# VectorE in a fixed order in the output projection, spatial gating in matmuls of 256 columns, LayerNorm stages further apart

## The chip, the core and the metric

The kernel runs on one core of a Trainium2 chip. Five engines matter here: TensorE (PE in the profile, with its weight loads as PEld), VectorE (DVE), ScalarE (ACT), GpSimd (POOL) and SyncE (SP), which issues all the DMAs of this kernel. The metric is the device time of one execution in microseconds; lower is better. Each engine works through its own list of instructions in order, and an instruction that must wait for another engine holds up everything behind it on its own.

## The reference

One layer of a streaming encoder with two branches of 512 channels each, over a prompt of 2048 frames and a sample of 32 frames. D_MODEL is 1024, all in float32.

```python
h = jnp.einsum('bsd,de->bse', x, w_in)            # 1024 -> 6 * 512
u, v, ga, bv, bg, gb = jnp.split(h, [...], axis=-1)
u = jax.nn.gelu(u, approximate=False)
v = layer_norm(jax.nn.gelu(v, approximate=False), a_ln_g, a_ln_b)
y_a = u * spatial_gating(v, a_ws, a_bias) * jax.nn.silu(ga)
a = bv * jax.nn.sigmoid(bg)
c, new_hist = depthwise_causal_conv(conv_hist, a, b_conv_w, b_conv_b)   # width 31
y_b = jax.nn.silu(layer_norm(c, b_ln_g, b_ln_b)) * jax.nn.silu(gb)
y = jnp.einsum('bse,ed->bsd', jnp.concatenate([y_a, y_b], axis=-1), w_out)
x_new = layer_norm(ALPHA * x + y, post_ln_g, post_ln_b)
```

`spatial_gating` multiplies each chunk of 128 positions, for each of 8 heads of 64 channels, by a lower triangular 128 x 128 matrix and adds a bias per position. The outputs are the new x of prompt and sample, the last 30 rows of the convolution's input of both, and the normalised v of the sample.

## The kernel before

*Precision.* TensorE is fed with a 32-bit format that rounds. So every operand is split into a high part (a rounding copy on ScalarE) and a low part (the difference, mostly on GpSimd, line 74, or VectorE, line 68), and a product is three matmuls: high by high, high by low, low by high. Splitting is much of ScalarE's and GpSimd's work.

*Stages.* The frames stand in four groups of 512 columns (the second has the 32 sample frames besides). They are treated in two halves p of two groups each. A half runs, in this order: v of its first group (`mm_v`, lines 328 to 330), the projections bg and bv (`mm_f`, lines 301 and 304), v of its second group, then u, ga and gb. Behind them comes the output projection (`o_tile`, `o_sample`, `o_product`, all through `mm`, line 664).

*The order of work.* A planner puts the instructions of each engine in an order ahead of time, by a due time that `when(t)` sets and by its own estimate of when operands are ready; a buffer is given out when its holder has been read for the last time. One unit of t is 12 matmuls of 512 columns. `chain(t, ...)` gives each of several functions a due time one unit after the last; `at(t, fn)` calls a function when the loop has come to t. `tc.issue_after(i)` fixes that what follows is queued behind i on the same engine. `mm` does so for every matmul of the output projection; the other engines' order there is the planner's.

*Spatial gating.* `ev_v` takes v of a group through GELU and its LayerNorm, splits it (tiles vh and vl, line 558), and lets `spat(u, two)` run for each pair of chunks u and each parity `two` of the heads: four heads, three matmuls of 128 columns each (line 573, weights from v, moving operand wth or wtl, the split triangular matrices), into one bank of PSUM, which ScalarE empties into S with two copies (line 578), one for each chunk. The sample's chunk takes 32 rows and 32 columns (tile wts). Units are two t apart.

*Branch B.* `conv` runs as chains of scalar-tensor-tensor instructions on VectorE (line 71). `ln_chain` then takes each group through six stages: sums of the channels, mean (by matmuls with ones, lines 441 and 442), squares, deviation and reciprocal, scaling (z), and SiLU with the gate (sw, gates). They are given to `chain`, one unit apart.

*Split of x.* `split_x` splits the transposed x; its low part is on VectorE for group 0 and on GpSimd for the others (line 183).

*Output projection.* The first two of eight units of 256 rows and the sample are plain products. Units 2 to 7 use a Strassen-like scheme of seven products in place of eight (`PRODUCTS`): of the blocks A11, A12, A21, A22 of y (unit's rows by channels) with S1 = A21 + A22, S2 = S1 - A11, S3 = A11 - A21, S4 = A12 - S2. Each product is 12 matmuls of 512 columns. Products 1, 3, 5 and 7 of a unit add up in one bank (oA), 2 in oB, 4 and 6 in oC. After each product VectorE reads the bank into the rows r of the result, so the next product into oA may start only when VectorE has read the one before. `load_yraw` brings the blocks of y from DRAM; `y_block` makes the four sums on VectorE (S2 is written over A11, so it waits until A11 is split), and splits each block for TensorE, five blocks ahead of use. `finish` then normalises each tile of 128 rows: inverse deviation by a power on GpSimd, r scaled and shifted on ScalarE, times the gain on VectorE, plus the bias on GpSimd, and the store.

In the last unit the first of its two tiles is finished in halves, one half on VectorE and one on GpSimd, and the last one in VectorE alone.

Of the kernel before, what the change touches and what calls it, by code (L numbers as in the profile page):

```python
# [15 lines left out]
P = 128  # L16
# [28 lines left out]
def hymba_step_kernel(ctx, tc, xT, xn, xs_n, wall, wsT, abias, vecs, avec, post, cache,  # L45
# [132 lines left out]
    def split_x(g, k):  # L178
        t = sb.tile([P, 2, WMAX], F32R, name=f"xs{g}_{k}", tag="xs", bufs=20)
        r = xraw.pop((g, k))  # L180
        w = GW[g]
        nc.scalar.copy(t[:, 0, :w], r[:, :w])  # L182
        (tt if g == 0 else gtt)(t[:, 1, :w], r[:, :w], f(t[:, 0, :w]), SUB)
        xsp[g, k] = t
# [41 lines left out]
    wts = sb.tile([NS, 2, 8, NS], F32R, name="wts", tag="pg", bufs=1)  # L226
# [26 lines left out]
    def setup_order():  # L253

        wm = setup["wm"]
        nc.scalar.copy(wts[:, 0], wm[:NS, :, :NS])
        tt(wts[:, 1], wm[:NS, :, :NS], f(wts[:, 0]), SUB)
# [4 lines left out]
    def setup_hi():  # L262
        for a in range(2):
            nc.scalar.copy(wt[0][:, :, 64 * a : 64 * a + 64], setup["wm"][:, :, a:P:2])

    def setup_lo():
        for a in range(2):
            c = slice(64 * a, 64 * a + 64)
            tt(wt[1][:, :, c], setup["wm"][:, :, a:P:2], f(wt[0][:, :, c]), SUB)

    def setup_bias():
        bb = setup["bb"]
        for h4 in range(2):
            p = bank(f"wsum{h4}")
            sl = slice(4 * h4, 4 * h4 + 4)
            nc.tensor.matmul(p, one1, wt[0][:, sl], start=True, stop=False)
            nc.tensor.matmul(p, one1, wt[1][:, sl], start=False, stop=True)
# [168 lines left out]
    def ln_chain(g, h):  # L446
# [45 lines left out]
        def run():  # L492
# [10 lines left out]
            chain(h, *fns)  # L503
# [23 lines left out]
    def ev_v(g, res):  # L527
# [33 lines left out]
        def spat(u, two):  # L561
# [3 lines left out]
            if (u, two) == (0, 0):  # L565
                S[g] = sb.tile([P, 4, WMAX], F32, name=f"S{g}", tag="S", bufs=2)
            p = bank(f"sp{g}_{u}_{two}")
            for pr in range(4):
                h = 2 * pr + two
                hi, lo = [x[:m, h, : len(ch), :] for x in sp[u]]  # L570
                o = p[:w, P * pr : P * pr + P]
                for m3, (l, r) in enumerate(((hi, 0), (hi, 1), (lo, 0))):
                    nc.tensor.matmul(o[:, :m], l, wt[r][:, h] if m == P else wts[:, r, h],  # L573
                                     start=(pr + m3 == 0), stop=(m3 == 2), skip_group_check=True)
# [90 lines left out]

    def load_wo(k, dh):
# [23 lines left out]
    def load_y(u):  # L690

        g, c0 = u // 2, 256 * (u % 2)
        for j in range(4):
# [6 lines left out]
            elif j % 2 == 0:  # L700
# [345 lines left out]
```

## Time and profile before

| | |
|---|---|
| three runs | 798.62, 802.79 and 1060.04 us, median 802.79 |
| the profiled execution | 797.06 us, of which the span from the first to the last instruction is 795.3 us |
| granted clock of TensorE, mean | 0.983 |
| chain that ended last | PE 73%, DMA 9%, DVE 7%, POOL 3% |
| matmuls of f (lines 301 and 304) | 2400, busy 591.7 us |
| matmuls of the output projection (line 664) | busy from 598.7 to 784.1 us |
| DMA | 101.18 MB, mean 127 GB/s |

Rows of groups give line, engine, operation, output <- inputs, shape and count, then busy time in us and mean ns of one, then the idle time before them. Rows in order of time give start and length in us, and in brackets the idle time of the engine just before and what ended it. Matmuls overlap, so their cost is read from one start to the next rather than from their length. Rows of windows give a stretch, its length, the busy time of PE, PEld, DVE, ACT and POOL with the number of instructions, and then TensorE's granted clock, the DMA engines' share and GB/s.

### The profile page before, as it was taken

What the parts mean: (1) busy time and instruction counts of PE and PEld (TensorE: products, weight loads), DVE (VectorE), ACT (ScalarE), POOL (GpSimd) and SP (SyncE); (2) the same over time, 40 slices, a digit from 0 to 9 for tenths busy, and PEclk for the clock granted to TensorE, in tenths of its full rate; (3) what the DMA queues carried; (4) which work ended last, traced back from release to release, by engine and by line L of the source; (5) the groups of instructions that cost most, each with busy time, mean ns of one, the idle gap of its engine ahead of it and who ended that gap; (6) DMA issues with size and microseconds to landing.
All of it is one profiled execution on the core that took longest, in us unless ns stands there. A gap on an engine that the chain in (4) does not pass through costs nothing.

```text
span 795.3 us, 10662 instructions
## 1 busy us (share of the span) xinstructions
PE 765.8 (96%) x3787; PEld 639.7 (80%) x3787; DVE 571.4 (72%) x842; ACT 303.3 (38%) x523; POOL 395.9 (50%) x337
## 2 busy tenths in 40 slices
PE   8999999999999899899999999999999999889894
PEld 6899998899889799788888888888887877678673
DVE  5449899899962667115999899984657577776675
ACT  5662332443223566463221254333546222233320
POOL 2654575545437834954132544332101565886673
PEclk9999999999989899999999999999999999999998
DMA  9631453312136733831111311123618888244112
GB/s 299 216 101 41 125 186 105 102 44 67 44 133 227 245 101 96 270 95 40 41 44 50 95 55 40 40 80 102 216 44 282 257 330 319 100 139 133 53 54 80
DMA packets 63718, 101.18 MB, mean 127 GB/s; under 512 B 8624, under 2 KB 30256, under 8 KB 63536
## 3 DMA queue, kind: packets, MB, share of 16 engines
q1 hardware_dynamic: 63664, 100.49, 38.8%
q8 instruction: 30, 0.49, 0.2%
q14 instruction: 24, 0.20, 0.1%
HBM read 74.32 MB, written 26.14 MB: 126 GB/s over the span
## 4 chain that ended last, share of the span: by engine, by line
PE 73%; DMA 9%; DVE 7%; POOL 3%; issue 3%; ACT 2%; SPq 1%; DVEq 0%; POOLq 0%; ACTq 0%
PE f L301 34%; PE f L304 17%; PE oA L664 6%; PE t L329 3%; PE t L330 3%; PE t L328 3%; DMA out_dram<-r 2%; PE sp L573 2%; DVE yr L68 2%; PE oB L664 2%; DMA yr<-yd 1%; DMA xr<-in_xT_dram 1%; DMA t3l<-td 1%; DVE gb L68 1%; DVE r L68 1%
## 5 line engine op out<-in xcount | busy, mean ns | idle before, releaser
L301 PE MATMUL f<-xs,wh 128*128 128x512 f32 (+2 forms) x1600 | 377.2, 359 | 0.0
L301 PEld LDWEIGHTS f<-xs,wh 128*128 128x128 f32 x1600 | 276.2, 191 | 41.3
L74 POOL TENSOR_TENSOR wl<-wr,wh 128x512 fp32r<-128x512 f32 x104 | 140.4, 1353 | 224.8 <-ACT wh L162 224.6
L304 PE MATMUL f<-xs,wl 128*128 128x512 f32 (+2 forms) x800 | 214.5, 357 | 0.0
L304 PEld LDWEIGHTS f<-xs,wl 128*128 128x128 f32 x800 | 144.2, 191 | 21.0
L162 ACT CAST wh<-wr 128x512 fp32r<-128x512 f32 x112 | 69.1, 620 | 183.8 <-PE f L301 84.8
L71 DVE SCALAR_TENSOR_TENSOR c<-A,hF,c 128x512 f32<-128x512 f32 x120 | 90.4, 753 | 6.3 <-ACT c L77 3.0
L71 DVE SCALAR_TENSOR_TENSOR c<-A,vec,c 128x512 f32<-128x512 f32 x120 | 89.7, 747 | 0.0
L71 DVE SCALAR_TENSOR_TENSOR c<-d,vec,c 128x512 f32<-128x512 f32 x112 | 83.6, 747 | 0.6
L329 PE MATMUL t<-wl,xs 128*128 128x512 f32 x128 | 50.3, 404 | 2.1 <-POOL wl L74 2.1
L328 PE MATMUL t<-wh,xs 128*128 128x512 f32 x128 | 48.2, 401 | 0.8 <-ACT xs L202 0.8
L330 PE MATMUL t<-wh,xs 128*128 128x512 f32 x128 | 48.3, 401 | 0.0
L74 POOL TENSOR_TENSOR r<-r,pgb 128x1024 f32<-128x1024 f32 (+1 forms) x16 | 38.4, 2402 | 17.8 <-DVE r L68 10.5
L74 POOL TENSOR_TENSOR xs<-xr,xs 128x512 fp32r<-128x512 f32 (+1 forms) x24 | 33.3, 1403 | 23.5 <-ACT xs L182 23.4
L68 DVE TENSOR_TENSOR A<-f,sg 128x512 f32<-128x512 f32 (+1 forms) x20 | 10.7, 579 | 36.6 <-PE f L304 35.4
L74 POOL TENSOR_TENSOR yl_A<-yr,yh_A 128x512 fp32r<-128x512 f32 x18 | 25.9, 1440 | 17.0 <-ACT yh_A L827 14.7
L578 ACT COPY S<-sp 64x512 f32<-64x512 f32 (+1 forms) x34 | 19.1, 562 | 35.6 <-PE sp L573 35.3
L74 POOL TENSOR_TENSOR to<-bo,to 128x256 fp32r<-128x256 f32 x32 | 26.3, 824 | 12.9 <-ACT to L361 12.8
L68 DVE TENSOR_TENSOR S<-S,ga 128x512 f32<-128x512 f32 (+1 forms) x16 | 13.8, 892 | 25.2 <-ACT ga L77 25.2
L361 ACT CAST to<-bo 128x256 fp32r<-128x256 f32 x32 | 12.9, 406 | 48.1 <-DMA td<-to 24.6
L329 PEld LDWEIGHTS t<-wl,xs 128*128 128x128 f32 x128 | 24.7, 193 | 8.0 <-POOL wl L74 2.5
L328 PEld LDWEIGHTS t<-wh,xs 128*128 128x128 f32 x128 | 24.7, 194 | 7.9 <-ACT xs L202 1.3
(179 smaller groups left out, 1200.1 us busy)
## 6 DMA issues: line engine op xcount, KB each, us to landing
wr<-in_wall_dram SPq DMA_DIRECT2D x112, 256.0 KB, 2.6
td<-to SPq DMA_DIRECT2D x32, 256.0 KB, 2.8
yr<-yd SPq DMA_DIRECT2D x64, 128.0 KB, 3.3
r<-in_xn_dram SPq DMA_DIRECT2D x16, 512.0 KB, 5.0
out_dram<-r SPq DMA_DIRECT2D x14, 512.0 KB, 2.6
xr<-in_xT_dram SPq DMA_DIRECT2D x23, 256.0 KB, 4.1
bo<-in_wall_dram SPq DMA_DIRECT2D x32, 128.0 KB, 2.8
wor<-in_wall_dram SPq DMA_DIRECT2D x16, 256.0 KB, 2.7
```

Source lines behind the costliest of these rows:

```text
L68: nc.vector.tensor_tensor(out, a, b, op=op)
L71: nc.vector.scalar_tensor_tensor(out, a, s, b, op0=op0, op1=op1)
L74: nc.gpsimd.tensor_tensor(out, a, b, op=op)
L162: nc.scalar.copy(hi, r)
L301: nc.tensor.matmul(pt[b][:, :w], hk, xsp[g, k][:, part, c0 : c0 + w], start=(k == 0 and part == 0), stop=False)
L304: order["mm"] = nc.tensor.matmul(pt[b][:, :w], lk, xsp[g, k][:, 0, c0 : c0 + w], start=False, stop=(k == NK - 1))
L328: nc.tensor.matmul(pt[t][:m], hi[:, c0 : c0 + m], wh, start=st, stop=False)
L329: nc.tensor.matmul(pt[t][:m], hi[:, c0 : c0 + m], wl, start=False, stop=False)
L330: nc.tensor.matmul(pt[t][:m], lo[:, c0 : c0 + m], wh, start=False, stop=en)
L573: nc.tensor.matmul(o[:, :m], l, wt[r][:, h] if m == P else wts[:, r, h], start=(pr + m3 == 0), stop=(m3 == 2), skip_group_check=True)
L578: nc.scalar.copy(S[g][64 * two : 64 * two + 64, :, c0 : c0 + m], p3[r, :, :m])
L664: order["mm"] = nc.tensor.matmul(out, l, r, start=start, stop=stop, skip_group_check=True)
```

## The change

1. *VectorE in a fixed order in the output projection.* A helper `dve` queues each VectorE instruction behind the one before. The reads of the banks, the statistics, the finishing steps and the sums of y all go through it. The sums are a function of their own (`y_sum`), called behind product 2 (S4 of this unit), 3 (S1), 5 (S2) and 6 (S3, the last three for the next unit). S2 has a buffer of its own instead of A11's. The product with the gain of a tile is put off into the next unit (`o_affine`, behind products 1 and 4), and its addition on GpSimd goes in two halves. `load_yraw` is called earlier, for the whole unit.
2. *Spatial gating in matmuls of 256 columns.* High and low part of the triangular matrices lie beside each other in one tile. A head is two matmuls, high and low part of v by both. A bank holds two heads; ScalarE copies the half that came from the high matrix, VectorE adds the other to it. There are twice as many units of half the size, one t apart.
3. *LayerNorm stages of branch B* are due at 0, 2, 4, 6, 7 and 8 units instead of 0 to 5.
4. The low part of x of group 3 moves from GpSimd to VectorE.
5. The last unit's finish is rewritten: its first tile is finished inside the last tile's sequence, and the last tile's additions are two halves instead of three parts.

```diff
@@ split_x
-        (tt if g == 0 else gtt)(t[:, 1, :w], r[:, :w], f(t[:, 0, :w]), SUB)
+        (tt if g in (0, 3) else gtt)(t[:, 1, :w], r[:, :w], f(t[:, 0, :w]), SUB)
@@ setup
-    wt = [sb.tile([P, 8, P], F32R, name=f"wt{x}", tag=f"wt{x}", bufs=1) for x in "hl"]
+    wt = sb.tile([P, 8, 2, P], F32R, name="wt", tag="wt", bufs=1)
@@ ln_chain
-            chain(h, *fns)
+            for dt, fn in zip((0, 2, 4, 6, 7, 8), fns):
+                when(h + dt)
+                fn()
@@ ev_v
-        def spat(u, two):
+        def spat(u, pr, two):
...
-            p = bank(f"sp{g}_{u}_{two}")
-            for pr in range(4):
-                h = 2 * pr + two
+            p = bank(f"sp{g}_{u}_{pr}_{two}").rearrange("p (q b) -> p q b", q=2)
+            for q in range(2):
+                h = 2 * (pr + q) + two
                 hi, lo = [x[:m, h, : len(ch), :] for x in sp[u]]
-                o = p[:w, P * pr : P * pr + P]
-                for m3, (l, r) in enumerate(((hi, 0), (hi, 1), (lo, 0))):
-                    nc.tensor.matmul(o[:, :m], l, wt[r][:, h] if m == P else wts[:, r, h],
-                                     start=(pr + m3 == 0), stop=(m3 == 2), skip_group_check=True)
-            p3 = p.rearrange("p (a b) -> p a b", a=4)
+                o = p[:w, q, : 2 * m]
+                both = wt[:, h] if m == P else wts[:, h]
+                nc.tensor.matmul(o, hi, both, start=True, stop=False)
+                nc.tensor.matmul(o, lo, both, start=False, stop=True)
             for j, (_, c0, _) in enumerate(ch):
                 r = slice(64 * j, 64 * j + 64)
-                nc.scalar.copy(S[g][64 * two : 64 * two + 64, :, c0 : c0 + m], p3[r, :, :m])
+                d = S[g][64 * two : 64 * two + 64, pr : pr + 2, c0 : c0 + m]
+                nc.scalar.copy(d, p[r, :, :m])
+                tt(d, p[r, :, m : 2 * m], d, ADD)
...
-        units = [(u, two) for u in range(3 if five else 2) for two in range(2)]
+        units = [(u, pr, two) for u in range(3 if five else 2) for pr in (0, 2) for two in range(2)]
         for j, a in enumerate(units):
-            at(h + 6 + 2 * j + (4 if a[0] else 0), lambda a=a: spat(*a))
-        at(h + 6 + 2 * len(units) + 4, spat_affine)
+            at(h + 6 + 2 * j // 2 + (4 if a[0] else 0), lambda a=a: spat(*a))
+        at(h + 6 + len(units) + 4, spat_affine)
@@ output projection
+    def dve(name, *a, **kw):
+        with tc.issue_after(order["dve"].ins) if "dve" in order else ExitStack():
+            order["dve"] = getattr(nc.vector, name)(*a, **kw)
...
+    def y_sum(u, n):
+        a11, a12, a21, a22 = [yraw[u, f"A{x}"] for x in ("11", "12", "21", "22")]
+        if n == "S1":
+            yraw[u, n] = sb.tile([P, 4, P], F32, name=f"ya{u}", tag="bo", bufs=2)
+            dve("tensor_tensor", yraw[u, n], a21, a22, op=ADD)
+        elif n == "S2":
+            d = sb.tile([P, W + HH + 1], F32, name=f"yb{u}", tag="dx", bufs=1)
+            yraw[u, n] = d[:, :W].rearrange("p (k n) -> p k n", k=4)
+            dve("tensor_tensor", yraw[u, n], yraw[u, "S1"], a11, op=SUB)
+        elif n == "S3":
+            yraw[u, n] = a21
+            dve("tensor_tensor", a21, a11, a21, op=SUB)
+        else:
+            yraw[u, n] = a12
+            dve("tensor_tensor", a12, a12, yraw[u, "S2"], op=SUB)
...
@@ o_product, after the matmuls of product j
-                stt(r[t][:, c], r[t][:, c], ALPHA, q)
+                dve("scalar_tensor_tensor", r[t][:, c], r[t][:, c], ALPHA, q, op0=MUL, op1=ADD)
             else:
-                tt(r[t][:, c], r[t][:, c], q, ADD)
-            when(t0 + 1 + n / 2)
+                dve("tensor_tensor", r[t][:, c], r[t][:, c], q, op=ADD)
             if j in (1, 4, 5, 6):
-                nc.vector.bn_stats(ost[t][:, dh + n, :], r[t][:, c])
+                dve("bn_stats", ost[t][:, dh + n, :], r[t][:, c])
...
+        if not (final and j == 6):
+            act(r[t], r[t], AF.Identity, bias=neg_mean_rstd(mv, r1, f"{u}_{t}"), scale=r1)
+            waiting_g[u, t] = (r[t], dst)
+            return
+        halves = [slice(0, W), slice(W, D)]
+        r1t, dst1 = waiting_g.pop((u, 1))
+        dve("tensor_tensor", r1t[:, :W], r1t[:, :W], pgb[:, 0, :W], op=MUL)
+        gtt(r1t[:, W:], r1t[:, W:], pgb[:, 0, W:], MUL)
+        gtt(r1t[:, W:], r1t[:, W:], pgb[:, 1, W:], ADD)
+        nc.sync.dma_start(dst1[:, W:], r1t[:, W:])
+        for c in halves:
+            dve("scalar_tensor_tensor", r[t][:, c], r[t][:, c], mv[:, 0:1], pgb[:, 0, c], op0=SUB, op1=MUL)
+        for c in halves:
+            dve("scalar_tensor_tensor", r[t][:, c], r[t][:, c], r1, pgb[:, 1, c], op0=MUL, op1=ADD)
+            nc.sync.dma_start(dst[:, c], r[t][:, c])
+        dve("tensor_tensor", r1t[:, :W], r1t[:, :W], pgb[:, 1, :W], op=ADD)
+        nc.sync.dma_start(dst1[:, :W], r1t[:, :W])
...
+    def o_affine(u, t):
+        r, dst = waiting_g.pop((u, t))
+        dve("tensor_tensor", r, r, pgb[:, 0], op=MUL)
+        for c in (slice(0, W), slice(W, D)):
+            gtt(r[:, c], r[:, c], pgb[:, 1, c], ADD)
+        nc.sync.dma_start(dst, r)
+
+    def extra(u, j):
+        v = u + 1 if u < 7 else None
+        if j in (0, 3) and (u - 1, j == 0) in waiting_g:
+            o_affine(u - 1, int(j == 0))
+        elif j == 1:
+            y_sum(u, "S4")
+        elif j in (2, 4, 5) and v:
+            y_sum(v, ("S1", None, "S2", "S3")[j - 2])
@@ the loop over units 2 to 7
-    for i, u in enumerate(units):
+    when(t - 9)
+    load_yraw(2)
+    when(t - 6)
+    for n in ("S1", "S2", "S3"):
+        y_sum(2, n)
+    for u in units:
...
+        if u < 7:
+            when(t - 4)
+            load_yraw(u + 1)
         for j in range(7):
             while ready < len(blocks_y) and ready - len(used) < 5:
-                v, n = blocks_y[ready]
-                if (v, "A11") not in yraw:
-                    when(t - 11 + j)
-                    load_yraw(v)
                 when(t + j - 8)
-                y_block(v, n)
+                y_block(*blocks_y[ready])
                 ready += 1
             o_product(u, j, t + j, u == units[-1])
             used.add((u, PRODUCTS[j][0]))
+            when(t + j + 1)
+            extra(u, j)
```

More of the change, by code (lines that the diff above doesn't have):

```diff
@@ L255, in setup_order @@
         wm = setup["wm"]
-        nc.scalar.copy(wts[:, 0], wm[:NS, :, :NS])
-        tt(wts[:, 1], wm[:NS, :, :NS], f(wts[:, 0]), SUB)
+        nc.scalar.copy(wts[:, :, 0], wm[:NS, :, :NS])
+        tt(wts[:, :, 1], wm[:NS, :, :NS], f(wts[:, :, 0]), SUB)
         nc.sync.dma_start(wmd, wm)
@@ L263, in setup_hi @@
         for a in range(2):
-            nc.scalar.copy(wt[0][:, :, 64 * a : 64 * a + 64], setup["wm"][:, :, a:P:2])
+            nc.scalar.copy(wt[:, :, 0, 64 * a : 64 * a + 64], setup["wm"][:, :, a:P:2])
     def setup_lo():
@@ L268, in setup_lo @@
             c = slice(64 * a, 64 * a + 64)
[L269 removed]
+            tt(wt[:, :, 1, c], setup["wm"][:, :, a:P:2], f(wt[:, :, 0, c]), SUB)
     def setup_bias():
@@ L275, in setup_bias @@
             sl = slice(4 * h4, 4 * h4 + 4)
-            nc.tensor.matmul(p, one1, wt[0][:, sl], start=True, stop=False)
-            nc.tensor.matmul(p, one1, wt[1][:, sl], start=False, stop=True)
+            nc.tensor.matmul(p, one1, wt[:, sl, 0], start=True, stop=False)
+            nc.tensor.matmul(p, one1, wt[:, sl, 1], start=False, stop=True)
             for hh in range(4):
@@ L699, in load_y @@
                 hl = [x4[:, 0], x4[:, 1]]
-            elif j % 2 == 0:
-                four = [sb.tile([P, 4, 256], F32R, name=f"y{x}{u}_{j}", tag=y, bufs=1)
-                        for x, y in zip("hl", (("vh", "vl"), ("wth", "wtl"))[j // 2])]
+            elif j == 0:
+                four = [sb.tile([P, 4, 256], F32R, name=f"y{x}{u}_{j}", tag="v" + x, bufs=1) for x in "hl"]
+            elif j == 2:
+                eight = sb.tile([P, 2, 4, 256], F32R, name=f"y{u}_{j}", tag="wt", bufs=1)
+                four = [eight[:, x] for x in range(2)]
             if u == 0:
@@ L730, in load_r, with neg_mean_rstd @@
         R[u] = r
+    def neg_mean_rstd(mv, r1, tag):
+        nm = sb.tile([P, 1], F32, name=f"on{tag}", tag="on1", bufs=4)
+        dve("tensor_scalar", nm, mv[:, 0:1], -1.0, None, op0=MUL)
+        gtt(nm, nm, r1, MUL)
+        return nm
     def finish(r, m, parts, dst, tag):
@@ L739, in finish @@
         gtt(r1[:m], r1[:m], mhalf[:m, :1], ALU.pow)
-        if parts["out"] == [slice(0, D)] and m == P:
-            nm = sb.tile([P, 1], F32, name=f"on{tag}", tag="on1", bufs=4)
-            nc.vector.tensor_scalar(nm, mv[:, 0:1], -1.0, None, op0=MUL)
-            gtt(nm, nm, r1, MUL)
-            act(r, r, AF.Identity, bias=nm, scale=r1)
-            if parts.get("halves"):
-                for row, op in ((0, MUL), (1, ADD)):
-                    tt(r[:, :W], r[:, :W], pgb[:, row, :W], op)
-                    gtt(r[:, W:], r[:, W:], pgb[:, row, W:], op)
-                    when(TEND + 90)
-                nc.sync.dma_start(dst[:, W:], r[:, W:])
-                nc.sync.dma_start(dst[:, :W], r[:, :W])
-                return
+        if m == P:
+            act(r, r, AF.Identity, bias=neg_mean_rstd(mv, r1, tag), scale=r1)
             tt(r, r, pgb[:, 0], MUL)
@@ new lines, in o_product @@
+        if j < 5:
+            return
+        mv = sb.tile([P, 2], F32, name=f"omv{u}_{t}", tag="omv", bufs=4)
+        r1 = sb.tile([P, 1], F32, name=f"or{u}_{t}", tag="or1", bufs=4)
+        dve("bn_aggr", mv, ost[t][:, : 1 + len(parts) if j == 6 else 2, :])
+        dve("tensor_scalar", r1, mv[:, 1:2], EPS, None, op0=ADD)
+        when(t0)
+        gtt(r1, r1, mhalf[:, :1], ALU.pow)
+        row = 256 * u + P * t
+        dst = y_p[row : row + P]
+        if not (final and j == 6):
+            act(r[t], r[t], AF.Identity, bias=neg_mean_rstd(mv, r1, f"{u}_{t}"), scale=r1)
+            waiting_g[u, t] = (r[t], dst)
+            return
```

31 lines of the change are left out of this document (11 added, 20 removed).

## The prediction

> **What bounds the kernel now.** I read the page first, for the engine that is always busy; then the view of who waited for whom, cut to TensorE (PE), for what interrupts it; then windows of busy time with the granted clock; then the order of time around the interruptions.
>
> ```profile
> span 795.3 us, 10662 instructions
> PE 765.8 (96%) x3787; PEld 639.7 (80%) x3787; DVE 571.4 (72%) x842; ACT 303.3 (38%) x523; POOL 395.9 (50%) x337
> ...
> PE oA L664 <- DVE r L68: 9.2, 5, 3.0
> PE t L329 <- POOL wl L74: 2.1, 1, 2.1
> PE var L441 <- ACT lr L480: 2.1, 1, 2.1
> ...
> PE var L442 <- DVE lr L68: 0.8, 1, 0.8
> ...
> PE oA L664 <- DVE r L71: 0.5, 1, 0.5
> ```
>
> PE is busy 96% of the span, so the time is PE's work, plus its few waits (total, times, longest), plus what follows its last matmul. The largest wait is the output projection's for VectorE (DVE). The clock is the second loss. It stands third from the end in these windows, the first, the longest and the last of five:
>
> ```profile
> 218.00:221.40 3.40, 3.40 (x12) 2.96 (x12) 1.76 (x3) 0.38 (x2) 0.00 (x0) 0.50 0.00 0
> ...
> 272.70:279.40 6.70, 5.94 (x20) 5.02 (x21) 6.26 (x6) 3.99 (x7) 6.62 (x7) 0.50 0.84 269
> ...
> 740.30:743.60 3.30, 3.30 (x9) 2.52 (x9) 1.35 (x5) 0.00 (x0) 0.74 (x2) 0.50 0.00 0
> ```
>
> Four times for 3.4 us and once for 6.7 PE ran at half its clock, 20 us in all, so 10 lost. Two of the windows (from 218.0 and from 228.3) lie in the spatial gating of the 32 sample rows, one in the LayerNorm of branch B, two (from 716.4 and from 740.3) in the projection, the last three right behind a pause of PE.
>
> **The projection (DVE in a fixed order).** What the 3.0 us wait is made of:
>
> ```profile
> 687.47 1.20 DVE L68 TENSOR_TENSOR ys<-yr,yr 128x512 f32<-128x512 f32 x1
> 688.59 2.88 DVE L68 TENSOR_TENSOR yr<-yr,yr 128x512 f32<-128x512 f32 x1
> 691.40 1.74 DVE L68 TENSOR_TENSOR yr<-yr 128x512 f32<-128x512 f32 x1
> 693.07 0.68 DVE L68 TENSOR_TENSOR r<-r,oA 128x512 f32<-128x512 f32 x1
> ...
> 690.22 0.39 PE L664 MATMUL oC<-t4l,yh_A 128*128 128x512 f32 x1
> 690.45 0.40 PE L664 MATMUL oC<-t4h,yl_A 128*128 128x512 f32 x1
> 693.89 0.70 PE L664 MATMUL oA<-wo,yh_S 128*128 128x512 f32 x2 [3.04 <-DVE r L68]
> ```
>
> The seventh product adds into the bank oA, which DVE must first have read after the fifth (the row at 693.07). That read stands behind three sums of y in DVE's queue. One 512-column matmul starts every 0.23 us (690.22 to 690.45), so a unit of 84 is 19.4 us and a product 2.77 us. The change lays DVE's order down: each read stands ahead of the sums, and the sums are spread, one behind the second, third, fifth and sixth product. S2 no longer overwrites A11 and so no longer waits for GpSimd's (POOL) split of it. Does DVE keep up? Its prices in this stretch:
>
> ```profile
> L860 DVE BATCH_NORM_STATS2 ost<-r 128x6 f32<-128x512 f32 x22 | 15.3, 694 | 0.7
> L68 DVE TENSOR_TENSOR r<-r,pgb 128x1024 f32<-128x1024 f32 x10 | 12.4, 1238 | 1.4 <-ACT r L77 1.4
> L68 DVE TENSOR_TENSOR yr<-yr,yr 128x512 f32<-128x512 f32 x4 | 11.5, 2883 | 0.6 <-POOL yl_A L74 0.6
> L71 DVE SCALAR_TENSOR_TENSOR r<-r,oA 128x512 f32<-128x512 f32 x15 | 10.2, 681 | 12.5 <-PE oA L664 12.5
> ...
> L737 DVE BATCH_NORM_AGGREGATE omv<-ost 128x2 f32<-128x12 f32 x10 | 2.1, 209 | 0.3
> ```
>
> Per unit: seven reads at 0.68 (4.8), four statistics at 0.69 (2.8), two products with the gain at 1.24 (2.5), some 1.0 of small ones (three for each of two tiles, the dearest 0.21), and the sums: S1 1.20, S4 2.88, S3 1.74, and S2, not in these rows, between a read's 0.68 and S1's 1.20; together 6.5 to 7.0. That is 18 us in a unit of 19.4: it fits, narrowly. Between the end of the first product and the start of the fifth, DVE reads three banks (2.0), takes one statistic (0.7), scales one tile (1.2) and forms S4 (2.9), 6.8 us where PE gives 8.3 from one end to the other; the scaled tile must first come through POOL and ScalarE (ACT), which eats the rest where it is late. POOL's and ACT's work per unit is as before. The eight loads of y per unit go earlier on SP's queue, past the stores of finished tiles; they are wanted from the third product on and their buffers come free a unit ahead, so I cost them at nothing. If they were late, the fixed order would now hold the reads behind them as well.
>
> The waits in oA (9.2 + 0.5) and the two half-clock windows (6.8 us, 3.4 lost) make 13.1 us. I leave 0.4 us a unit, near the smallest of today's waits (0.5): **-10.7**. Ends: -13.1, and -3 if the DVE stays the bound.
>
> **Spatial gating, full chunks.** Per head three matmuls of 128 columns become two of 256: 192 become 128.
>
> ```profile
> 55.15 0.45 PE L301 MATMUL f<-xs,wh 128*128 128x512 f32 x1
> 55.44 0.22 PE L573 MATMUL sp<-wtl,vh 128*128 128x128 f32 x1
> 55.49 0.28 PE L573 MATMUL sp<-wth,vl 128*128 128x128 f32 x1
> 55.61 0.44 PE L301 MATMUL f<-xs,wh 128*128 128x512 f32 x1
> ...
> 57.48 0.28 PE L304 MATMUL f<-xs,wl 128*128 128x256 f32 x1
> 57.60 0.30 PE L301 MATMUL f<-xs,wh 128*128 128x288 f32 x1
> ```
>
> The first of two occupies 0.05 us (55.44 to 55.49), the second 0.12 (to 55.61), and the 512-column matmul behind such a group takes 0.29 (55.15 to 55.44) instead of 0.23: every one of them costs 0.11 in the end, a group of one too (0.05 + 0.06), which looks like a weight load that a short matmul can't cover. So 192 x 0.11 = 21.1 us. At 256 columns a start takes 0.12 (57.48 to 57.60) with nothing left over: 128 x 0.12 = 15.4. **-5.7.** Ends: -5.7, and 0 if the 0.06 of delay stays.
>
> **The 32 sample rows.** 24 matmuls of 32 columns become 16 of 64.
>
> ```profile
> 214.07 0.23 PE L573 MATMUL sp<-wts,vh 32*64 32x32 f32 x1
> 214.23 0.38 PE L301 MATMUL f<-xs,wh 128*128 128x256 f32 x1
> 214.54 0.23 PE L573 MATMUL sp<-wts,vh 32*64 32x32 f32 x1
> ```
>
> Each takes 0.16, and its 256-column neighbour 0.31 instead of 0.12: 0.35 together, of which the width is a small part. Eight fewer: **-2.8** (ends -2.8, -1.5). Twelve spread over a half step, twice, bring the first two half-clock windows. The twelve become eight, with half as many units between: I take one window gone, 3.4 us at half, **-1.7** (ends 0, -3.4). The Trainium skill, "TensorE: Matmul & The Clock Gate", Part 1, has the clock follow PE's activity in free-running windows of about 3.4 us; these windows' length agrees. By it which window falls in a stretch of stalls is chance, and the two would go or stay independently.
>
> **Emptying the gating's banks.** One half of the bank is copied by ACT, the other added by DVE:
>
> ```profile
> L68 DVE TENSOR_TENSOR A<-f,sg 128x256 f32<-128x256 f32 x4 | 1.5, 416 | 0.0
> ...
> 100.00:235.00 135.00, 135.00 (x764) 116.57 (x763) 121.90 (x192) 46.72 (x96) 66.34 (x62) 0.97 0.30 97
> ```
>
> ACT's 32 copies of 512 columns become 64 of 256, 0.41 each by the cast of that width at 265.00 below, 26 us on an engine that is 38% busy. DVE gets 64 adds of 256 columns out of PSUM at 0.42, 27 us, and four small ones. While the convolution runs (100 to 235) DVE is busy 122 of 135 us, so its end moves by up to the 15 us of two groups. PE doesn't wait for the convolution's end today, and what it feeds (branch B's gate) is wanted only after the next group of projections: 0 us, covered by PE's own 135 us here. Without that cover the price is those 15 us in each half. Each bank is also held one DVE turn longer (0.74 us for a convolution step, then two adds).
>
> **Split of x for the fourth group, POOL to DVE.** Eight subtractions leave the queue that made PE wait for wl:
>
> ```profile
> 325.70 5.08 POOL L74 TENSOR_TENSOR xs<-xr,xs 128x512 fp32r<-128x512 f32 x4 [0.47 <-ACT xs L182]
> 330.72 2.52 POOL L74 TENSOR_TENSOR wl<-wr,wh 128x512 fp32r<-128x512 f32 x2
> ```
>
> Four of them stand right ahead of wl, 5.1 us against a wait of 2.1. On DVE they are some 0.7 each and behind the gates of branch B. **-2.1** (ends -2.1, and +2 if DVE is late with them).
>
> **LayerNorm stages further apart.** The stages' due times go from 1 to up to 2 steps apart, 3 steps later at the end. What is late there is not a due time:
>
> ```profile
> 265.00 0.41 ACT L361 CAST to<-bo 128x256 fp32r<-128x256 f32 x1 [1.38 <-DMA td<-to]
> 265.31 1.21 ACT L77 ACTIVATE ls<-A 128x544 f32<-128x544 f32 x2
> ```
>
> The squares stand in ACT's queue behind a cast that waits for a DMA, and PE then waits 2.1 + 0.8 us with 6.7 us of half clock behind it, 6.2 in all. I see nothing that takes that cast away: **0** (ends -6.2, and +3 for a fuller DVE).
>
> **The end.**
>
> ```profile
> 784.11 0.42 DVE L71 SCALAR_TENSOR_TENSOR r<-r,oA 128x256 f32<-128x256 f32 x1 [1.20 <-PE oA L664]
> ...
> 788.21 1.75 DVE L68 TENSOR_TENSOR r<-r,pgb 128x512 f32<-128x512 f32 x1
> 789.88 1.53 DVE L71 SCALAR_TENSOR_TENSOR r<-r,or,pgb 128x512 f32<-128x512 f32 x3
> ```
>
> Behind PE's last matmul (784.1) DVE works until 791.4. Its last three additions become two of a half each (1.4 at twice a read's 0.68), and of the first tile's two half products, slowed beside POOL like the 1.75 here, I let one run at 1.0: **-0.8** (ends -2 with both at 0.7, and +1 where the store behind them waits).
>
> **Sum**: -10.7 - 5.7 - 2.8 - 1.7 - 2.1 - 0.8 = -23.8. The profiled execution took 797.1 us (795.3 and 1.8 around it), so 773.3; the runs shown lie above it (798.6, and 802.8 as the median), and I add 1.7: **775**.
>
> **Rivals.**
> *DVE stays the bound of the projection.* For: 18 of 19.4 us, and the sums slowed whenever POOL runs: yr<-yr,yr took 2.88 at 688.59, and took it four times out of four. The Trainium skill, "SBUF — State Buffer", section "Who interferes with whom", says that a DVE instruction with two SBUF inputs contends with a POOL one that reads SBUF; by that rule, which these rows bear out, moving the sums doesn't make them cheaper. Against: no read stands behind three sums any more. Every unit 1.6 us too long (9.6) and both windows of half clock (3.4), less the 2.4 counted: **785**.
> *The gating's matmuls don't do what they say*: each 256-column one still delays its neighbour, and both windows stay. 775 + 5.7 + 1.7 + 2: **784**. Against: the row at 57.48.
> *LayerNorm's wait goes after all*: 775 - 6.2: **769**.
> *Slower: PE waits for banks.* The gating's 36 banks, twice today's 18, come free only when DVE has added. Six banks are shared with the projection's f, which takes three at a time. If at each of today's 18 half steps PE waits out a copy (0.4), a convolution step (0.75) and two adds (0.84), it loses 36 us: **811**. It ends above 797 from 1.3 us per half step. Against: PE waits for no such bank today.
>
> **Chances.** Forecast (766 to 781) 0.56, LayerNorm 0.08, DVE bound 0.19, gating 0.12, slower 0.05. The range 764 to 788 leaves out the slower case and the outer edges of the others. About 2% (16 us, so below 783) is what a measurement of this kernel tells from no change: faster 0.56 + 0.08 + a quarter of the next two, 0.72; within 2% 0.24; slower 0.04.
>
> **What would show it.** The wait of oA for r should be nearly gone and a unit near 19.4 us; no half clock between 700 and 780; sp x128, with 0.12 from start to start; no PE wait for wl; PE still waiting for lr. Wrong if PE waits for f, t or sp on DVE's adds, if the reads of oA stand behind a tile that ACT hasn't scaled, or if waits for y appear on DVE.

## The result, and the profile after

The changed kernel took 765.88 us (median of 4 runs, 764.03 to 766.93), the kernel before, beside it on the same chip, 801.95 (median of 4, 798.62 to 1060.04). The ratio is 0.956, with a 95% interval of 0.952 to 0.960, from which the slow run of 1060.04 us is left out: 36 us faster by the medians, 35 without that run. The forecast was 775 in a range of 764 to 788. The profiled execution took 766.93 us. Between the two profiled executions the span fell by 30.1 us only, because the one profiled before (797.06) was faster than any of the timed ones and the one profiled after was the slowest of its four; the accounts below are of these 30.1.

The page of the changed kernel gives its span and the busy time of the engines:

```profile
span 765.2 us, 10630 instructions
PE 745.7 (97%) x3715; PEld 623.4 (81%) x3715; DVE 588.0 (77%) x917; ACT 307.6 (40%) x557; POOL 400.9 (52%) x339
```

PE does less work (745.7 us, 20 fewer than before) and waits less, and its share of the chain that ended last goes from 73% to 83%. The view of who waited for whom, cut to PE, of the changed kernel:

```profile
PE var L441 <- ACT lr L480: 2.2, 1, 2.2
...
PE f L304 <- POOL wl L74: 1.0, 1, 1.0
PE f L301 <- ACT gv L77: 1.0, 1, 1.0
...
PE oA L667 <- DVE r L672: 0.9, 1, 0.9
PE mu L441 <- ACT lr L480: 0.9, 1, 0.9
PE var L442 <- DVE lr L68: 0.6, 1, 0.6
PE t L329 <- POOL wl L74: 0.6, 1, 0.6
```

The 9.7 us in oA are down to one wait of 0.9, in the very last product. LayerNorm's wait for lr is still there. One window of half clock is left inside PE's work, of 3.4 us, behind that wait (270.9 to 274.6, with a clock of 0.54 in the mean, in the view of windows); before there were 20 us of them.

One unit of the projection, before and after, in the view of windows (length, busy time of PE, PEld, DVE, ACT, POOL, then clock, DMA share, GB/s). The first row is the kernel before, second is one of the changed kernel:

```profile
671.30:693.90 22.60, 19.56 (x85) 15.70 (x85) 17.66 (x25) 6.84 (x9) 17.40 (x14) 1.00 0.29 94
```

```profile
657.50:676.80 19.30, 19.30 (x85) 15.68 (x84) 14.03 (x23) 6.61 (x9) 18.94 (x16) 1.00 0.33 106
```

PE works without a gap, 19.3 us per unit, where the forecast had 19.4 and 0.4 of waits. DVE, feared at 18 us, needs 14. POOL is busy 19 of 19.3 us: beside PE it is now the engine with no room.

Where the 30.1 us came from, stage by stage (the start of the same matmul of f or of the projection, counted from the first, in both traces):

| stage | before, us | after, us | gain | forecast |
|---|---|---|---|---|
| first 864 matmuls of f, with the gating of groups 0 and 1 | 205.1 | 204.3 | 0.9 | with the p = 1 row: 5.7 |
| f 865 to 1009: the 32 sample rows | 35.1 | 26.1 | 9.0 | 2.8 + 1.7 |
| f 1010 to 1441: LayerNorm of branch B, turn to the second half | | | 0.9 | 0 + 2.1 for x |
| f 1441 to 2113: second half with its gating | | | 3.3 | (above) |
| rest, and start of the projection | | | 1.7 | 0 |
| six units of seven products | 130.9 | 118.3 | 12.5 | 10.7 |
| behind PE's last matmul | 11.3 | 9.5 | 1.8 | 0.8 |

The 0.9 of the first row is not the gating's. The first matmul of f starts at 24.1 us in the one execution and at 22.7 in the other; from there on the stage took 181.0 us before and 181.6 after. In the twelve kernels profiled here f starts either at 22.3 to 22.7 or at 24.1 to 24.7, and PE waits for wl or gv soon after only in the four where it starts early. Why it starts early in some was not followed.

### The profile page after: what moved, and what is told of

Its sections match the earlier page's. It is cut to its first block, busy times and chain, and to the rows that moved or that the text cites. A ratio compares the mean times of both kernels' runs of the same rounds, so it can differ in the third digit from the quotient of the medians.

```text
span 765.2 us, 10630 instructions
## 1 busy us (share of the span) xinstructions
PE 745.7 (97%) x3715; PEld 623.4 (81%) x3715; DVE 588.0 (77%) x917; ACT 307.6 (40%) x557; POOL 400.9 (52%) x339
## 4 chain that ended last, share of the span: by engine, by line
PE 83%; DMA 5%; DVE 4%; POOL 3%; issue 2%; ACT 2%; SPq 0%; DVEq 0%; POOLq 0%; ACTq 0%
PE f L301 35%; PE f L304 17%; PE oA L667 9%; PE o L667 4%; PE oC L667 4%; PE t L329 2%; PE t L330 2%; PE t L328 2%; PE oB L667 2%; POOL wl L74 1%; DMA xr<-in_xT_dram 1%; PE sp L576 1%; PE sp L575 1%; PE os L667 1%; POOL xs L74 1%
## 5 line engine op out<-in xcount | busy, mean ns | idle before, releaser
L301 PE MATMUL f<-xs,wh 128*128 128x512 f32 (+2 forms) x1600 | 370.8, 352 | 1.0 <-ACT gv L77 1.0
L74 POOL TENSOR_TENSOR wl<-wr,wh 128x512 fp32r<-128x512 f32 x104 | 143.8, 1385 | 218.2 <-ACT wh L162 212.2
L74 POOL TENSOR_TENSOR r<-r,pgb 128x512 f32<-128x512 f32 (+1 forms) x26 | 42.2, 1636 | 9.2 <-DVE r L68 5.1
L68 DVE TENSOR_TENSOR S<-sp,S 64x256 f32<-64x256 f32 (+1 forms) x68 | 27.8, 409 | 19.1 <-ACT S L580 17.3
L667 PE MATMUL o<-wo,y 128*128 128x512 f32 x144 | 34.7, 396 | 0.3 <-DVE wo L68 0.2
L580 ACT COPY S<-sp 64x256 f32<-64x256 f32 (+1 forms) x68 | 24.4, 359 | 24.9 <-PE sp L576 14.1
L74 POOL TENSOR_TENSOR xs<-xr,xs 128x544 fp32r<-128x544 f32 (+1 forms) x16 | 21.8, 1368 | 22.3 <-ACT xs L182 22.1
L667 PEld LDWEIGHTS o<-wo,y 128*128 128x128 f32 x144 | 26.9, 188 | 7.4 <-DVE wo L68 1.1
L77 ACT ACTIVATE r<-r,on,or 128x1024 f32<-128x1024 f32 x15 | 18.7, 1246 | 34.7 <-POOL on L74 34.7
```

Source lines behind the costliest of these rows:

```text
L68: nc.vector.tensor_tensor(out, a, b, op=op)
L74: nc.gpsimd.tensor_tensor(out, a, b, op=op)
L77: nc.scalar.activation(out, in_, func, bias=bias, scale=scale)
L301: nc.tensor.matmul(pt[b][:, :w], hk, xsp[g, k][:, part, c0 : c0 + w], start=(k == 0 and part == 0), stop=False)
L580: nc.scalar.copy(d, p[r, :, :m])
L667: order["mm"] = nc.tensor.matmul(out, l, r, start=start, stop=stop, skip_group_check=True)
```

## The experiments

Each run stands beside runs of the kernel before on the same chip. Ratios are to those, with a 95% interval.

**1. The projection alone**, in the kernel before: parts 1 and 5 of the change (`dve`, `y_sum`, `o_affine`, `extra`, the last unit's finish, `load_yraw` moved), and nothing else.

> The kernel before with the output projection's part alone: VectorE in the fixed order, sums of y spread, S2 in a buffer of its own, the new finish. Theory (the projection's gain is its own, and needs none of the other parts): the six units take 118 us instead of 130.9, no half clock in them, and the time falls by 13 to 16 us (projection 12.5, end 1.8, up to 1.7 at its start). Rival (part of the gain comes from the other parts, since work left over from branch B would otherwise stand in VectorE's way): 10 us or less.

783.76 us against 800.18, ratio 0.978 (0.976 to 0.981), 16.4 us less. The view of who waited for whom, for PE in this kernel:

```profile
PE var L441 <- ACT lr L480: 2.5, 1, 2.5
PE t L329 <- POOL wl L74: 2.0, 1, 2.0
...
PE oA L664 <- DVE r L669: 0.9, 1, 0.9
```

The waits in oA went but for one by this part alone; wl and lr stayed. In the trace its six units are 11.3 us shorter, and what follows PE's last matmul 1.5. One new wait stands in the units, 0.9 us in oC for a load of the sums of w_out (t4l); the changed kernel does not have it. The rest of the 16.4 is again the profiled run of before being short (span 795.3 to 782.5 is 12.9).

**2. The gating alone**, in the kernel before: part 2 of the change. LayerNorm's spacing, the split of x and the projection are as before.

> The kernel before with the gating in matmuls of 256 columns alone. Theory (the sample's matmuls cost a switch for each group of them, and the groups get fewer): 11 to 14 us less, some 9 of them where the sample's gating stands (before: from 210 to 235 us), no half clock there. Rival (as in the prediction's sum: eight matmuls fewer at 0.35 us, and chance for the clock): 6 to 9 us less. Rival on the other side (PE waits for banks that VectorE still has to add): PE waits named sp or f for VectorE's adds, and less than 5 us gained.

779.5 us, ratio 0.974 (0.971 to 0.977), 20.7 less, twice the forecast's steps for this part (5.7, 2.8 and 1.7, together 10.2) and more than the 11 to 14 expected. In the trace the sample's stretch gained 9.0 us and the second half 3.3, just as in the whole change, the first 864 matmuls of f 2.0 and the start of the projection 2.0. The view of waits of this kernel shows that the projection changed as well, though no line of it was edited, since the planner ordered its VectorE work differently:

```profile
PE oA L665 <- DVE r L68: 3.8, 3, 3.3
PE oC L665 <- DVE r L71: 2.5, 2, 1.3
...
PE oA L665 <- DVE r L71: 0.8, 3, 0.5
```

That is 7.1 us against 9.7, and the six units are 3.3 us shorter, which this kernel got by the planner's luck. The projection and the gating alone sum to 37.1 us (33.8 without that), the split of x, in neither, adds some 3 (experiment 7), and the whole gave 35 to 36: about additive.

**3. The fixed order, taken out of the changed kernel.**

```diff
-        with tc.issue_after(order["dve"].ins) if "dve" in order else ExitStack():
-            order["dve"] = getattr(nc.vector, name)(*a, **kw)
+        getattr(nc.vector, name)(*a, **kw)
```

> The changed kernel without the fixed order on VectorE: the same instructions, buffers and due times, but the planner sorts VectorE in the projection. Theory (the order itself takes the waits away): reads of oA stand behind sums of y again, PE waits for r between 4 and 10 us in all, at least one half-clock window from 640 us on, and the time rises by 5 to 13 us. Rival (the sums spread by due time, and S2 in its own buffer, are enough): within 2 us of the changed kernel.

776.1 us, ratio 0.969 (0.965 to 0.972), 10 us more than the changed kernel. The view of waits (PE) and, below it, the order of time on DVE in a unit of this kernel:

```profile
PE oA L667 <- DVE r L672: 8.5, 4, 4.5
```

```profile
696.32 1.67 DVE L672 TENSOR_TENSOR ya<-yr,yr 128x512 f32<-128x512 f32 x1 [5.73 <-POOL yl_A L74]
698.02 1.63 DVE L672 TENSOR_TENSOR yr<-yr 128x512 f32<-128x512 f32 x1
699.58 0.68 DVE L672 TENSOR_TENSOR r<-r,oA 128x512 f32<-128x512 f32 x1
```

DVE stands still for 5.73 us with a sum whose operands are late, takes two sums, and only then reads the bank for which PE waits. (The bracket names POOL's split, which ends at 696.22. SP's order of time shows that four loads of y into the tiles of the sum are issued only from 691.24 on; which of the two ended the wait is not told apart.) The same functions with the same operands, in the fixed order (changed kernel, order of time on DVE):

```profile
685.38 0.69 DVE L672 SCALAR_TENSOR_TENSOR r<-r,oA 128x512 f32<-128x512 f32 x1 [0.38 <-PE oA L667]
685.98 0.72 DVE L672 TENSOR_TENSOR ya<-yr 128x512 f32<-128x512 f32 x1
688.13 0.69 DVE L672 SCALAR_TENSOR_TENSOR r<-r,oC 128x512 f32<-128x512 f32 x1 [1.42 <-PE oC L667]
...
690.90 0.69 DVE L672 TENSOR_TENSOR r<-r,oA 128x512 f32<-128x512 f32 x1 [0.71 <-PE oA L667]
```

Every read here waits for PE (the brackets), not PE for a read. The six units took 128.3 us without the order, 118.3 with it and 130.9 in the kernel before. So 10.0 of the 12.5 us are the order's. The other 2.5 are there without it, in a kernel that keeps the sums' buffers and the halved additions; which of these gave them was not tried.

**4. S2 over A11 again**, in the changed kernel, S3 ahead of S2 and both behind product 5.

```diff
-            d = sb.tile([P, W + HH + 1], F32, name=f"yb{u}", tag="dx", bufs=1)
-            yraw[u, n] = d[:, :W].rearrange("p (k n) -> p k n", k=4)
-            dve("tensor_tensor", yraw[u, n], yraw[u, "S1"], a11, op=SUB)
+            yraw[u, n] = a11
+            dve("tensor_tensor", a11, yraw[u, "S1"], a11, op=SUB)
...
-        elif j in (2, 4, 5) and v:
-            y_sum(v, ("S1", None, "S2", "S3")[j - 2])
+        elif j in (2, 4) and v:
+            for n in (("S1",), (), ("S3", "S2"))[j - 2]:
+                y_sum(v, n)
```

In unit 2 the sums are formed ahead of A11's split here, so its product with A11 is formed from S2; the amount of work is the same.

> The changed kernel with S2 written over A11 again, in the fixed order; S3 must then come ahead of S2, both behind the fifth product. Theory (A11 is split two products earlier, so the buffer of its own is worth little once the order is fixed): within 2 us of the changed kernel. Rival (VectorE waits for GpSimd's split of A11 and holds the reads up): VectorE waits for yl of 1 us and more in each unit, PE waits for r, 4 us or more.

766.02 us, ratio 0.956 (0.953 to 0.960): the same as the changed kernel. PE waits 1.0 once for POOL's split. The buffer of its own is worth nothing once the order is fixed.

**5. The sample's matmuls over 128 rows.** In the kernel before, the sample's triangular matrices and its v stand in tiles of 128 rows, zero behind the 32, so that the 24 matmuls are as tall as their neighbours. They stay 24 and 32 columns wide.

```diff
-    wts = sb.tile([NS, 2, 8, NS], F32R, name="wts", tag="pg", bufs=1)
+    wts = sb.tile([P, 2, 8, NS], F32R, name="wts", tag="pg", bufs=1)
...
+        nc.gpsimd.memset(f(wts), 0.0)
...
-                hi, lo = [x[:m, h, : len(ch), :] for x in sp[u]]
+                hi, lo = [x[:, h, : len(ch), :] for x in sp[u]]
```

> The kernel before with the sample's 24 gating matmuls on all 128 rows (rows 32 to 127 are zeros on both sides), still 32 columns each and still scattered. Theory (what costs 0.35 us is the switch between 128 and 32 rows, 0.19 going in): the 512 and 256 column matmuls ahead of them take their usual 0.23 and 0.12, each sample matmul costs 0.12 or less, and both half-clock windows go: 7 to 10 us less. Rival (a narrow matmul costs that much whatever its rows, or the clock falls by chance): 0 to 3 us less, and the same 0.19.

795.53 us, ratio 0.993 (0.991 to 0.996), 4.6 less. The stretch of time itself, in windows, first of the kernel before and then of this one:

```profile
205.20:240.20 35.00, 35.00 (x182) 28.59 (x181) 26.82 (x41) 9.77 (x21) 12.32 (x10) 0.90 0.31 108
```

```profile
205.20:240.20 35.00, 35.00 (x234) 31.82 (x233) 32.32 (x44) 13.00 (x29) 18.63 (x17) 1.00 0.46 141
```

In the same 35 us PE gets through 234 matmuls instead of 182, at full clock instead of 0.90. From one start to the same start the stretch is 8.4 us shorter. In order of time (PE, this kernel), two lone sample matmuls:

```profile
218.64 0.65 PE L305 MATMUL f<-xs,wl 128*128 128x512 f32 x3
219.13 0.18 PE L577 MATMUL sp<-wts,vh 128*64 128x32 f32 x1
219.15 0.47 PE L302 MATMUL f<-xs,wh 128*128 128x512 f32 x1
219.47 0.18 PE L577 MATMUL sp<-wts,vh 128*64 128x32 f32 x1
```

The three of f ahead take 0.49 us, as they do anywhere (0.48), the sample matmul itself 0.03, and the 512 columns behind it 0.32 (219.15 to 219.47) instead of 0.23. So a lone one costs 0.11 us here, where one cost 0.35 in the kernel before. That is as much as a lone one of 128 columns costs in the prediction's rows (0.05 + 0.06): the change from 128 rows to 32 and back makes 0.24 of the 0.35, and the rest is a short matmul's price, at 32 columns as at 128. The planner also packed the 24 closer, into 13 groups instead of 21, so the stretch's gain is not the rows' alone; the price of a lone one is.

By the medians 4.6 of the 8.4 us stayed; between the two profiled executions almost all was lost again later. LayerNorm's stage is 3.7 us longer (in this kernel's view of waits PE waits 5.4 us for lr). The six units are 4.5 longer, because the waits in oA are 10.8 us instead of 9.7 and four half-clock windows fall there instead of two.

**6. LayerNorm's spacing alone**, in the kernel before.

```diff
-            chain(h, *fns)
+            for dt, fn in zip((0, 2, 4, 6, 7, 8), fns):
+                when(h + dt)
+                fn()
```

> The kernel before with the LayerNorm stages' due times alone (0, 2, 4, 6, 7, 8). Theory (these instructions are overdue when their operands come, so later due times move little): within 2 us of the kernel before, PE still waits for lr. Rival (the spacing takes the wait away): no wait of PE for lr, the half clock behind it gone, 4 to 6 us less.

799.4 us, ratio 0.998 (0.996 to 1.001): no difference. PE waits 3.8 us for lr instead of 2.1. In the changed kernel the spacing does nothing: with it taken out, every engine's list of instructions comes out the same.

**7. The split of x for the fourth group back on POOL**, in the changed kernel.

```diff
-        (tt if g in (0, 3) else gtt)(t[:, 1, :w], r[:, :w], f(t[:, 0, :w]), SUB)
+        (tt if g == 0 else gtt)(t[:, 1, :w], r[:, :w], f(t[:, 0, :w]), SUB)
```

> The changed kernel with the low part of x of group 3 on GpSimd again. Theory (as predicted, GpSimd's queue makes wl late there): PE waits 2 us or more for wl between 305 and 330 us, where the changed kernel waits 0.6, and the time rises by 1.5 to 3 us. Rival (the new gating order has moved that stage already; the run of the gating alone showed a wait of 0.9 for wl): within 1 us.

768.93 us, ratio 0.960 (0.957 to 0.964): 3 us more by the medians, but the interval overlaps that of the changed kernel, so the size is not settled. At the turn to the second half the changed kernel waits 0.6 us for wl and for nothing else. This one waits for gb (1.7), wh (1.3) and wl (0.9), and the stage from f 1010 to 1441 is 2.5 us longer (103.8 against 101.3). Experiment 2, which also leaves this split on POOL, waits for the same three (1.7, 0.6, 0.9). The span is 1.5 us longer (766.7 against 765.2), since the changed kernel's execution had lost 1.0 in the first stage. The direction and the size in the stage are those of the forecast's 2.1; but two of the three waits are for ACT, and how POOL's split makes those was not followed.

**8. The casts of `wo_sums` moved**, in the changed kernel. These add blocks of w_out for the Strassen-like scheme: four of the eight stood in the time in which LayerNorm of branch B runs. They are put off by 50 units, with their loads and POOL's additions.

```diff
-        at((24 + 6 * j) if j < 4 else (54 + 4 * j), lambda j=j: after_w(wo_sums, j // 2, j % 2))
+        at((24 + 6 * j) if j < 4 else (104 + 4 * j), lambda j=j: after_w(wo_sums, j // 2, j % 2))
```

> The changed kernel with the last four of the eight steps that form sums of the output weights called 50 units later, in the second half, away from the LayerNorm of the first. Theory (ScalarE is held by their casts, which wait for GpSimd and DMAs, so the LayerNorm's squares are late): PE's waits for lr, 3.7 us in all, and the half-clock window behind them go, 3 to 5 us less. Rival (the chain from the mean to the deviation is as long as that by itself): the wait stays within 1 us of 2.2, and the time too.

759.76 us, ratio 0.948 (0.946 to 0.951), 6.3 less than experiment 4, which ran on the same chip. In order of time ACT, of the changed kernel and then of this one:

```profile
258.68 0.63 ACT L182 CAST xs<-xr 128x512 fp32r<-128x512 f32 x1 [3.34 <-DMA xr<-in_xT_dram]
...
261.23 1.21 ACT L77 ACTIVATE ls<-A 128x544 f32<-128x544 f32 x2
264.29 0.41 ACT L361 CAST to<-bo 128x256 fp32r<-128x256 f32 x1 [1.86 <-POOL bo L74]
...
268.62 0.65 ACT L480 CAST lr<-ls 128x544 fp32r<-128x544 f32 x1 [1.21 <-DVE ls L68]
```

```profile
252.34 0.62 ACT L182 CAST xs<-xr 128x512 fp32r<-128x512 f32 x1 [2.12 <-DMA xr<-in_xT_dram]
...
254.90 1.22 ACT L77 ACTIVATE ls<-A 128x544 f32<-128x544 f32 x2
...
261.74 0.65 ACT L480 CAST lr<-ls 128x544 fp32r<-128x544 f32 x1 [1.43 <-DVE ls L68]
```

In the changed kernel the squares (ls) stand behind a cast that waits 3.34 us for a load, and a cast of `wo_sums` (line 361) that waits for POOL parts them. The first of the two is a cast of x (line 182), not one that was moved: here it still waits 2.12 us, but comes 6.3 us earlier. With `wo_sums` gone from here the squares start 6.3 us earlier, and lr is ready before PE comes to it. PE's waits for lr and the half clock behind them are gone. How much of it is the casts' place on ACT, and how much the loads and additions that went with them, was not told apart.

**9 and 10. All that helped, together**, and experiment 8 again beside it: the moved casts, the sample over 128 rows, and the last product's bank read in one piece instead of two (`parts = [slice(0, W)]`).

> The changed kernel with the four casting steps moved, the sample's gating matmuls on 128 rows (zeros below row 32), and the last product in one piece of 512 columns. Theory: the sample's remaining switches (some six groups at 0.4 us) save 1 to 2 us, and the last product saves PE's wait of 0.9 for VectorE against one longer read, 0.3 to 0.6; together 1.5 to 2.5 us less than with the moved casts alone. Rival (each moves other work about as much as it saves, as the zeros did in the kernel before): within 1 us of it.

> The changed kernel with the four casting steps moved, once more beside the last version on the same chip: 0.946 to 0.951 of the kernel before, no PE wait for lr.

757.48 us (756.98 to 758.60, 6 runs), ratio 0.945 (0.943 to 0.947), and 759.0 (758.51 to 760.25) for the moved casts alone, ratio 0.947 (0.944 to 0.949). The two sets of runs touch at 758.5 to 758.6 and the intervals overlap, so the 1.5 us between them is likely but not established. In the trace the sample's stretch gave 1.55. The last wait in oA of 0.9 went and the units are 1.2 shorter, but what follows PE's last matmul is 1.2 longer: the one piece gained nothing. Two waits of 1.0 came back early on (gv and wl); f starts early in this execution.

## Why the forecast came out, point by point

**The projection, -10.7: the mechanism was right, 12.5 measured.** The queue of sums ahead of the read was the wait, and the order removed it (experiment 3 gives 10 us back by removing only that). I had left 0.4 us of waits per unit, and there are none but the last 0.9. The loads of y, costed at nothing, are nobody's wait in the changed kernel. *DVE stays the bound* did not happen, and its price was wrong. I took today's price of the sums (S4 2.88, S3 1.74) as theirs in any place. The groups on DVE during the projection of the changed kernel:

```profile
L672 DVE TENSOR_TENSOR r<-r,pgb 128x1024 f32<-128x1024 f32 x10 | 14.2, 1423 | 0.0
...
L672 DVE TENSOR_TENSOR yr<-yr,yb 128x512 f32<-128x512 f32 x6 | 5.9, 983 | 0.0
L672 DVE TENSOR_TENSOR yb<-ya,yr 128x512 f32<-128x512 f32 x5 | 4.4, 872 | 0.0
L672 DVE TENSOR_TENSOR yr<-yr 128x512 f32<-128x512 f32 x5 | 3.4, 682 | 0.0
```

S4 takes 0.98, S2 0.87, S3 0.68 and S1 about 0.7: 3.2 us for what I put at 6.5 to 7.0. Only the product with the gain rose, from 1.24 to 1.42. In the kernel before, S4 at 688.59 lay beside this one on POOL, in order of time:

```profile
688.09 2.84 POOL L74 TENSOR_TENSOR r<-r,pgb 128x1024 f32<-128x1024 f32 x1
```

S4 ended at 691.47, 0.54 us after that addition. In the changed kernel S4 still meets POOL's addition in every unit but the first, in order of time on DVE and on POOL (the latter in two windows, one for each half):

```profile
683.97 1.03 DVE L672 TENSOR_TENSOR yr<-yr,yb 128x512 f32<-128x512 f32 x1
```

```profile
683.15 1.30 POOL L74 TENSOR_TENSOR r<-r,pgb 128x512 f32<-128x512 f32 x1
684.40 1.75 POOL L74 TENSOR_TENSOR r<-r,pgb 128x512 f32<-128x512 f32 x1
```

S4 ends at 685.00, 0.55 us after the first half, which had started before it; the second half, started behind it, takes 1.75 instead of 1.30. The Trainium skill, "SBUF — State Buffer", section "Who interferes with whom", says that such a sum contends with a POOL instruction that reads SBUF, and that the order of issue decides which of the two is held up; these rows agree. S2 behaves the same (0.93 at 692.23, with a half that ends at 692.61). So for S4 the rival's rule was right, moving it did not keep it clear of POOL: it is cheaper because it now waits for half an addition and not a whole one, a part of the change that I had given no price. S1 and S3 are cheaper by their places, where no addition or split on POOL is far from its end. In experiment 3, with the halves but without the order, S1 and S3 met POOL's splits and took 1.67 and 1.63, and each ended 0.55 after the split that had started before it.

**Full chunks, -5.7: right in the matmul's price.** In order of time on PE in the changed kernel, the last of a row of such matmuls, with three of f behind it:

```profile
56.83 0.28 PE L576 MATMUL sp<-wt,vl 128*128 128x256 f32 x1
56.95 0.62 PE L301 MATMUL f<-xs,wh 128*128 128x512 f32 x2
57.41 0.39 PE L304 MATMUL f<-xs,wl 128*128 128x512 f32 x1
```

It takes 0.12 to the next start, and of the three of 512 behind it two take 0.46, so 0.23 each, with no delay. By stages 0.9 and 3.3 came, and about 1.0 more lies in the sample's stretch (it holds 12 of these matmuls before, 3 after): 5.2. The 0.9 is the early start of f and the two waits for wl and gv that came with it. In experiment 2, where f starts as late as in the kernel before and nothing waits, the first stage is 2.1 us shorter from the first matmul of f on, and the sum is 6.4. *The gating doesn't do what it says* is thereby out.

**The sample rows, -2.8, and their clock, -1.7: the step that was mis-sized.** I read 0.35 us off a lone matmul and took it for every one of the 24, so that eight fewer saved eight times that. Experiment 5 shows that most of it is the price of a switch between 128 and 32 rows. It is paid once for a group of sample matmuls that follow each other. Before there were 21 groups (18 lone ones and three pairs); in the changed kernel there are six, of two, four and two in each half step. In order of time on PE, the first half step:

```profile
211.32 0.41 PE L304 MATMUL f<-xs,wl 128*128 128x256 f32 x2
211.66 0.30 PE L575 MATMUL sp<-wts,vh 32*64 32x64 f32 x2
211.89 0.38 PE L301 MATMUL f<-xs,wh 128*128 128x256 f32 x1
212.20 0.30 PE L576 MATMUL sp<-wts,vl 32*64 32x64 f32 x2
...
212.54 0.40 PE L301 MATMUL f<-xs,wh 128*128 128x288 f32 x1
212.87 0.30 PE L576 MATMUL sp<-wts,vl 32*64 32x64 f32 x2
213.10 0.52 PE L301 MATMUL f<-xs,wh 128*128 128x256 f32 x2
213.45 0.41 PE L304 MATMUL f<-xs,wl 128*128 128x256 f32 x2
```

The two of f ahead of the first group (256 and 288 columns) take 0.34 instead of 0.25, the two behind the last one 0.35, and the ones between two groups 0.31 and 0.33 instead of 0.12 and 0.13: 0.09 on the matmul ahead of a group and 0.10 on the one behind. The groups themselves take 0.23, 0.34 and 0.23. So the six cost 6 x 0.19 + 2 x (0.23 + 0.34 + 0.23) = 2.7 us. Before, 21 groups cost 21 x 0.19, and 18 lone ones 0.16 and three pairs 0.21 each: 7.5, not 24 x 0.35 = 8.4. That is 4.8 saved, not 2.8. Both half-clock windows went, 3.4 and not 1.7. The stretch's 9.0, less the 1.0 of full chunks, is 8.0 against 8.2 by this sum. *LayerNorm's wait goes* did not happen; much of the time that brought the result below that rival's 769 came from here.

**Emptying the banks, 0: right.** The group on DVE for it, and DVE's busy time from 100 to 235 us in the windows, of the changed kernel:

```profile
L68 DVE TENSOR_TENSOR S<-sp,S 64x256 f32<-64x256 f32 (+1 forms) x68 | 27.8, 409 | 19.1 <-ACT S L580 17.3
```

```profile
100.00:235.00 135.00, 135.00 (x798) 118.57 (x798) 130.68 (x214) 50.60 (x112) 70.98 (x66) 1.00 0.35 107
```

27 us were forecast and 27.8 came; DVE is busy 130.7 of 135 us there and PE all 135. No wait of PE names S or a bank of the gating, so the slower rival's mechanism did not occur. The cover is nearly used up: 4.3 us of DVE are left in this stretch.

**LayerNorm's spacing, 0: right, and its reason in the main.** The squares do stand behind casts on ACT that wait for loads and for POOL, and what removed the wait was to take casts, loads and additions away from there (experiment 8), for 6.3 us. I had worked out 6.2 for the kernel before; in the changed kernel the three waits (2.2, 0.9 and 0.6) and half of the 3.4 us window make 5.4, so the agreement is in part chance.

**Split of x, -2.1: right in direction** (experiment 7), 2.5 in its stage in one pair of executions, not settled in size by the medians.

**The end, -0.8: 1.8 measured**, between the ends given (-2 and +1).

**Not in the list**: the projection's start, 1.7 us. There PE waits 1.4 us for ACT's split of wo (line 670) in the kernel before, and not in the changed one. Experiment 2 gained 2.0 there by the gating alone.

**The sum.** The terms came to 23.8 and 30.1 were measured; the sample's step is 3.5 of the 6.3 between them, the projection's units 1.8, its start 1.7, the end 1.0, less 1.7 for the full chunks and x together, which the early waits and LayerNorm's stage hid in this pair of executions. The 1.7 us added because the profiled run of before lay under its median did not recur: the changed kernel's profiled run is the slowest of its four. So 765.88 lies 9 us below the forecast and 2 above the lower end of the range, and just below the 766 to 781 that I had given the largest chance. Nearly all the misses point the same way, towards too small a gain, so the forecast did not come this near by errors that cancelled.

## What to carry to other kernels

When a producer waits for a bank, read the consumer's queue in order of time and lay down the order of that one engine, reads first: here this was worth 10 us with every instruction the same, and a buffer of its own for S2 was worth nothing on top. A small matmul's cost should be read from the starts of its neighbours, and tested by changing one thing about it; here two thirds of it was the number of rows, and padding with zeros or grouping removed that. Where two engines hold each other up, a shorter instruction on the one shortens the other's wait. A stage that is late was not cured here by its own due time: look at what stands in front of it on its engine and waits for something else.

## What the runs showed of the hardware

- A matmul of 32 rows alone among matmuls of 128 rows cost 0.35 us: 0.09 on the one ahead, 0.16 itself and 0.10 on the one behind. With zeros up to 128 rows it cost 0.11 (0.03 itself, 0.09 behind). The scattered ones brought two windows of half clock although the records show PE with no idle time there (35.00 of 35.00 us busy at a mean clock of 0.90). The Trainium skill, "TensorE: Matmul & The Clock Gate", Part 2, says of the weight load that the number of rows doesn't matter to its time; the records agree (64 columns of weights took 128 to 130 ns at 32 rows in the median, 137 to 138 at 128), so the cost lies in the change of height and not in the load's own length.
- A DVE sum with both inputs in SBUF (0.66 to 0.69 us alone) ended 0.54 to 0.55 us after the POOL instruction that had started before it: it took 2.88 beside a whole addition of 2.84 and 1.03 beside a half of 1.30. A POOL half that started behind the sum took 1.75 instead of 1.30.
